# Gates of mixer B by blocks of 64 channels on half of TensorE's rows, in a two-layer hybrid encoder

## The chip, the cores and the metric

The kernel runs on one core of one Trainium2 chip. The metric is the device time of one execution in microseconds (us). The core's engines are TensorE (PE in the profile, its weight loads PEld), VectorE (DVE), ScalarE (ACT), GpSimd (POOL, unused here) and SyncE (SP, which issues most DMAs). Each takes its instructions in the order of the program.

## The reference, cut to what matters

Two layers, 512 tokens, 1024 channels, float32. A layer projects the normalised input for four token mixers (A and C: grouped attention; D: dilated attention in three groups; B: a bidirectional gated linear recurrence), gates and sums their outputs, and ends with an MLP. Mixer B has 512 channels in 8 blocks of 64, and its gates are block diagonal:

```python
xh = xc.reshape(b, s, LRU_BLOCKS, LRU_BLOCK_W)            # 8 blocks of 64 channels
gl = einsum('bsnc,gncd->gbsnd', xh, gate_w) + gate_b      # g: the two gates
r, i = sigmoid(gl[0]), sigmoid(gl[1])
log_a = -8 * r * softplus(-lam); a = exp(log_a)
u = sqrt(-expm1(2 * log_a)) * (i * xc)                    # then h = a * h_before + u
```

This is done for a forward and a backward scan (`d`), each with its own gate weights, biases and `lam`.

## The kernel before, in words

Activations lie channels on partitions, tokens along the free axis, so most products are 128x128 weights against 128x512. For accuracy every matrix is split in a high and a low part (`fp32r`), and a product is three: high by high, high by low, low by high (`mm3`, lines 173 to 182: 177, 178, 179).

The weights come as a stream of chunks of 128x1024 in the order of `PLAN`: a DMA on SP (`wload`, line 102), a cast on ACT for the high part (`whi`, line 118), a subtraction on DVE for the low part (`wlo`, line 127). Three raw and three split chunks are held. `ahead` casts the next chunks when a chunk is taken; `lows` emits the subtractions after a group's products.

`phase1` makes the projections of a layer one group after the other (`group`, lines 385 to 395): 24 products into one PSUM tile, then pieces of mixer B that wait in a queue (`tick`, as many as `TICKS` says), then, after the groups that `GATES` names, the gates of a tile of 128 channels of mixer B. Tile 0 follows the first half of the second query group of mixer C, tile 1 the first half of D's query group 0, tile 2 and tile 3 the first and second half of D's key group 1. PSUM tiles come from three tags in turn (`wide`, line 165: mm, s, t), each with two buffers. Two projections together make a rotary (`rope`, lines 331 to 365: four products with the tables on DVE, line 338, reading both PSUM tiles, then sums, line 361, and DMAs to DRAM, line 363), so the first PSUM tile of a pair is held until after the second.

`gates_b` (lines 598 to 667) does the gates of tile f: four times (two scan directions by two gates) three products of a block-diagonal 128x128 weight, half of it zeros, with the tile's convolved input, and one tanh on ACT with the bias (line 619), which reads 128x512 from PSUM. What follows is queued as `s1` to `s6`: tanh, exp and square on ACT (lines 628 to 630), products on DVE (636, 637), a square root on ACT (642), the scan on DVE (648), sums (652, 653), and the split of the result (654 on ACT, 657 on DVE). The GeLU branch puts line 591 (tanh, ACT) and line 594 (DVE) in the same queue. Both gate tiles f and f+1 use one chunk of weights, `BG`.

After the projections come the values of A and C, then mixer A's attention, whose keys and queries are loaded back from DRAM (lines 769, 773) and whose first score product is line 786. The order on every engine is the order of this program.

Of the kernel before, what the change touches and what calls it, by code (L numbers as in the profile page):

```python
# [11 lines left out]
F32 = mybir.dt.float32  # L12
F32R = mybir.dt.float32r
I32 = mybir.dt.int32
AF = mybir.ActivationFunctionType
ALU = mybir.AluOpType
AX = mybir.AxisListType
PSUM = bass.MemoryType.PSUM
# [10 lines left out]
V_GMIX, V_GMLP, V_GB, V_CW, V_CB, V_LGB, V_LAM, V_G, V_SINK = 0, 8, 16, 48, 64, 68, 84, 92, 96  # L29
NV = 104  # L30
# [4 lines left out]
# attention of A and C: the stages of a step and how many steps each lags behind the first  # L35
# [4 lines left out]
# steps of an attention phase, steps of its fill, steps of the fill ahead of the first one  # L40
MG = ((35, 48, 3), (41, 73, 2), (18, 47, 12))
# waits in the end of mixer D, in steps of the fill beside it, and the steps of that fill
E1, E2, E3, FN = (1, 5, 2, 15)
# products that warm the tensor engine up; parts in which the first two chunks come
WU, P0, P1 = (16, 2, 2)
# the order of the projections; pieces of mixer B after each; projections that its gates follow
# [25 lines left out]
PLAN = layer_plan()  # L72
# [3 lines left out]
class Body:  # L76
# [29 lines left out]
    def parts(self, i):  # L106
        """the first chunk is worked on in parts, for an early start"""
        n = (P0, P1, 1)[min(i, 2)]
        return [slice(p * (1024 // n), (p + 1) * (1024 // n)) for p in range(n)]
# [20 lines left out]
    def ahead(self, i):  # L130
        """the high parts of the next groups, and the loads beyond them"""
        i -= self.held
        n = len(self.order)
        while self.n_split < min(i + self.HLB, n):
            self.whi()
        while self.n_load < min(self.n_lo + self.RAWB, n):
            self.wload()
# [5 lines left out]
    def take2(self, *key):  # L143
        """two chunks that stay for several groups"""
        return [self.take(*key, u, wide=u) for u in range(2)]
# [38 lines left out]
    def several(self, keys, mv, cuts):  # L184
        """the groups of some chunks, side by side: each part of the depth for all of them"""
        sts = [self.wst(self.take(*key, wide=u)) for u, key in enumerate(keys)]
        pss = [self.wide() for _ in keys]
        mm = self.nc.tensor.matmul
        for k0, k1 in zip((0,) + cuts, cuts + (KD,)):
            for st, ps in zip(sts, pss):  # L190
                for k in range(k0, k1):
                    (sh, sl), (mh, ml) = st(k), mv(k)
                    mm(ps, sh, mh, start=(k == 0), stop=False)
                    mm(ps, sh, ml, start=False, stop=False)
                    mm(ps, sl, mh, start=False, stop=(k == KD - 1))
        self.ahead(self.n_take)
        self.lows()
        return pss
# [19 lines left out]
    def smt(self, n, tag):  # L218
        return self.sm.tile([128, n], F32, tag=tag, name=tag)

    def rsqrt(self, v, n, tag):
        """v: [128, n] in SBUF, positive"""
        nv = self.nc.vector
        y, t = self.smt(n, tag + "y"), self.smt(n, tag + "t")
        yi = y.bitcast(I32)
        nv.tensor_scalar(out=yi, in0=v.bitcast(I32), scalar1=1, scalar2=None, op0=ALU.logical_shift_right)
        nv.tensor_scalar(out=yi, in0=yi, scalar1=-1.0, scalar2=float(0x5F3759DF), op0=ALU.mult, op1=ALU.add)
        for _ in range(3):
            nv.scalar_tensor_tensor(out=t, in0=y, scalar=-0.5, in1=y, op0=ALU.mult, op1=ALU.mult)
            nv.tensor_tensor(out=t, in0=t, in1=v, op=ALU.mult)  # L230
            nv.scalar_tensor_tensor(out=y, in0=t, scalar=1.5, in1=y, op0=ALU.add, op1=ALU.mult)
        return y

    def xg_tile(self, xt, c, gcol):
        """xt [128, 512] f32: tile c of the residual; writes xg"""
        nc = self.nc
        nc.scalar.activation(out=self.xh[:, c], in_=xt, func=AF.Copy, scale=gcol)
        nc.vector.scalar_tensor_tensor(
            out=self.xl[:, c], in0=xt, scalar=gcol, in1=self.xh[:, c].bitcast(F32), op0=ALU.mult, op1=ALU.subtract
        )  # L240
# [10 lines left out]
    def norm_cols(self):  # L251
        """1/rms of each token, as columns [128, 4]"""
        nc = self.nc
        ps = self.misc()
        for c in range(4):
            nc.tensor.matmul(ps[:, c:c + 1], self.acc[:, c * 128:(c + 1) * 128], self.ones[:, 0:1])
        v = self.smt(4, "nv")
        nc.vector.tensor_scalar(out=v, in0=ps[:, 0:4], scalar1=1.0 / DM, scalar2=EPS, op0=ALU.mult, op1=ALU.add)
        return self.rsqrt(v, 4, "n")
# [17 lines left out]
    def setup(self):  # L277
        nc = self.nc
# [14 lines left out]
        self.d_lgb = cp.tile([128, nl, 16], F32, name="d_lgb")  # L293
# [4 lines left out]
    def derive(self):  # L298
# [5 lines left out]
        ts(out=self.d_lgb, in0=vv[:, :, V_LGB:V_LGB + 16], scalar1=0.5, scalar2=None, op0=ALU.mult)  # L304
        ts(out=self.d_nsink, in0=vv[:, :, V_SINK:V_SINK + 8], scalar1=-1.0, scalar2=None, op0=ALU.mult)
        # softplus(-lam) = max(-lam, 0) + log1p(exp(-|lam|)), log1p(u) = 2 atanh(u / (u + 2))
        n = DEPTH * 8
        sh = lambda t: t.rearrange("p (l n) -> p l n", l=DEPTH)
        lam = self.smt(n, "spl")
        ts(out=sh(lam), in0=vv[:, :, V_LAM:V_LAM + 8], scalar1=1.0, scalar2=None, op0=ALU.mult)  # L310
        mx, u, d, s, s2, p = (self.smt(n, "sp" + c) for c in "mudsqp")
# [18 lines left out]
    # ================= projections of the mixers, and mixer B =================  # L330
    def rope(self, X1, X2, T, dst, split, perm=False):
        """X1, X2 in PSUM; T: the factors (of x1, of x2 in the first half; of x2, of x1 in the second)"""
# [64 lines left out]
    def phase1(self, l):  # L397
# [27 lines left out]
        def head_scale(key, nh, sel, n=128):  # L425
            """1/rms of each head and token, but for the token's own factor: [128, 4 * nh]"""
# [21 lines left out]
        # the tokens' 1/rms, as columns, as a row, and over all partitions  # L448
# [12 lines left out]
        # tokens in other orders: by 64 from 64 on for the first group of D, by residues for the others  # L461
# [47 lines left out]
        # queries of C, queries and keys of D; gates of mixer B between them  # L509
# [18 lines left out]
    def values_ac(self):  # L528
        """values of A and C: token-major, [hi | lo]"""
# [68 lines left out]
    def gates_b(self, f):  # L598
        """gates of a tile of mixer B; what follows goes to the queue"""
# [9 lines left out]
        Tg = {}  # L609
        for d in range(2):  # L610
            for gate in range(2):
                ps = self.wide()
                o = ((f % 2) * 4 + d * 2 + gate) * 128
                st = lambda k: (hl[0][:, o:o + 128], hl[1][:, o:o + 128])
                mv = lambda k: (xch[f][:, 0], xch[f][:, 1])
                self.run(self.mm3(ps, st, mv, 1))
                t = p1.tile([128, S], F32, tag=("btr", "bti")[gate], name="btg", bufs=4)
                i = (d * 2 + gate) * 4 + f
                ns.activation(out=t, in_=ps, func=AF.Tanh, scale=0.5, bias=self.d_lgb[:, l, i:i + 1])
                Tg[f, d, gate] = t  # L620
        bs = {}
# [11 lines left out]
        def s2(f, d):  # L633
            q, a, u = bs[f, d]
            # 1 - a^2 = tanh(-log a) (1 + a^2)
            nv.scalar_tensor_tensor(out=q, in0=Tg[f, d, 0], scalar=1.0, in1=q, op0=ALU.add, op1=ALU.mult)
            nv.scalar_tensor_tensor(out=u, in0=u, scalar=1.0, in1=self.xcs[f], op0=ALU.add, op1=ALU.mult)
# [61 lines left out]
    # ================= gates and projections of the branches =================  # L699
# [44 lines left out]
    # ================= attention =================  # L744
    def pipeline(self, steps, order):
        """steps: dicts of stages; order: (stage, its distance in steps from the first)"""
# [7 lines left out]
    def attn_gqa(self, l, which, y):  # L754
        """8 heads, 2 key heads. A: all keys; C: a band, with sinks"""
# [274 lines left out]
    def attn_d_end(self, y):  # L1030
        """the groups' weights: exp(m_g - M) / sum_g l_g exp(m_g - M)"""
# [57 lines left out]
    def merge(self, a, b, na, nb, first=0):  # L1089
        """a's first step, a few of b, then na steps of a spread over nb of b; then the rest"""  # L1090
# [19 lines left out]
    # ================= the layer =================  # L1110
    def layer(self, l):
# [99 lines left out]
        def last(h):  # L1211
            """the last two tiles and the final norm, by halves of the tokens"""
# [118 lines left out]
def _pack_weights(i):  # L1331
# [13 lines left out]
    for l in range(DEPTH):  # L1345
# [3 lines left out]
        for key in PLAN:  # L1349
# [19 lines left out]
            elif k == "BG":  # L1369
                c = np.zeros((128, 8, 128), np.float32)  # L1370
                for f in range(2):
                    for d in range(2):
                        for g in range(2):
                            for h in range(2):
                                s = slice(64 * h, 64 * h + 64)
                                c[s, f * 4 + d * 2 + g, s] = gw[d, g, (2 * a[0] + f) * 2 + h]
# [15 lines left out]
def _pack_vectors(i):  # L1392
# [3 lines left out]
    for l in range(DEPTH):  # L1396
# [6 lines left out]
        v[:, V_LGB:V_LGB + 16] = i["lru_gate_b"][l].reshape(16, 128).T  # L1403
        v[:, V_LAM:V_LAM + 8] = i["lru_lambda"][l].reshape(8, 128).T
# [63 lines left out]
```

## Time and profile before

| | us |
|---|---|
| median of 3 runs | 2096.09 |
| lowest and highest run | 2095.13, 2098.7 |
| span of the profiled execution | 2091.4 |
| TensorE busy | 2071.0 (99%) |
| DVE busy | 1273.3 (61%) |
| ACT busy | 977.9 (47%) |

The span runs from the first to the last instruction of one profiled execution; the profile gives no other time of that execution, and the runs, taken without a profile, have medians 4.7 us above the span. Times in rows are counted from the start of the span. Busy times of TensorE are modelled from starts, since products overlap; the distance from start to start is the rate.

### The profile page before, as it was taken

How to read it: one execution, taken by the hardware profiler on the slowest of the kernel's cores; microseconds unless marked ns; L12 is line 12 of the kernel's file. 1: busy time of each engine (PE TensorE's matmuls, PEld its weight loads, DVE VectorE, ACT ScalarE, POOL GpSimd, SP SyncE). 2: the span in 40 equal slices, each digit the busy share in tenths (PEclk: the TensorE clock that was granted, in tenths of full speed). 3: DMA queues.
4: the chain of work that ended last, by engine and by line, in shares of the span. 5: the costliest groups of instructions: out<-in, count | busy, mean ns of one | idle time of the engine just before them, and what ended most of it. 6: DMA issues, size and time to landing. Idle time of an engine off the chain costs nothing.

```text
span 2091.4 us, 25718 instructions
## 1 busy us (share of the span) xinstructions
PE 2071.0 (99%) x9800; PEld 1711.7 (82%) x9800; DVE 1273.3 (61%) x2274; ACT 977.9 (47%) x1703; POOL 0.2 (0%) x4
## 2 busy tenths in 40 slices
PE   9999999999999999999999999999999999999997
PEld 7888889987778888888878888898877788888886
DVE  6889774575466544444658887736644665444445
ACT  4366885663534332322323667757545343322322
POOL 0000000000000000000000000000000000000000
PEclk9999999999999999999999999999999999999999
DMA  5445313122234222222325552312321432223221
GB/s 190 156 142 159 113 54 100 59 97 95 72 100 144 95 97 94 97 93 99 133 95 171 159 163 67 101 66 66 121 81 53 135 117 93 99 93 99 93 100 61
DMA packets 83407, 220.74 MB, mean 106 GB/s; under 512 B 15674, under 2 KB 17850, under 8 KB 83284
## 3 DMA queue, kind: packets, MB, share of 16 engines
q1 hardware_dynamic: 80404, 214.91, 31.6%
q10 hardware_dynamic: 2880, 4.20, 0.6%
q8 instruction: 77, 1.26, 0.3%
q14 instruction: 46, 0.38, 0.1%
HBM read 197.94 MB, written 21.12 MB: 105 GB/s over the span
## 4 chain that ended last, share of the span: by engine, by line
PE 96%; DVE 2%; ACT 1%; issue 1%; DMA 0%; SPq 0%; DVEq 0%; ACTq 0%
PE ps_mm L177 15%; PE ps_mm L179 14%; PE ps_mm L178 14%; PE ps_t L177 6%; PE ps_t L179 6%; PE ps_t L178 6%; PE ps_s L177 6%; PE ps_s L179 6%; PE ps_s L178 6%; PE ps_o L846 2%; PE ps_t L825 2%; PE ps_s L786 1%; PE ps_s L787 1%; PE ps_o L992 1%; PE ps_t L966 1%; PE ps_s L917 1%
## 5 line engine op out<-in xcount | busy, mean ns | idle before, releaser
L118 ACT CAST whi<-raw 128x1024 fp32r<-128x1024 f32 (+1 forms) x318 | 329.9, 1042 | 353.6 <-PE ps_mm L178 122.0
L127 DVE TENSOR_TENSOR wlo<-raw,whi 128x1024 fp32r<-128x1024 f32 (+1 forms) x318 | 385.0, 1214 | 106.0 <-ACT whi L118 103.3
L177 PE MATMUL ps_mm<-xh,whi 128*128 128x512 f32 x720 | 288.2, 400 | 0.0
L179 PE MATMUL ps_mm<-xh,wlo 128*128 128x512 f32 x720 | 282.0, 392 | 0.0
L178 PE MATMUL ps_mm<-xl,whi 128*128 128x512 f32 x720 | 281.8, 391 | 0.0
L177 PEld LDWEIGHTS ps_mm<-xh,whi 128*128 128x128 f32 x720 | 135.5, 188 | 32.4 <-issue 4.1
L179 PEld LDWEIGHTS ps_mm<-xh,wlo 128*128 128x128 f32 x720 | 135.6, 188 | 29.3
L178 PEld LDWEIGHTS ps_mm<-xl,whi 128*128 128x128 f32 x720 | 135.8, 189 | 26.9
L177 PE MATMUL ps_t<-xh,whi 128*128 128x512 f32 x368 | 143.7, 390 | 0.0
L178 PE MATMUL ps_t<-xl,whi 128*128 128x512 f32 x368 | 143.2, 389 | 0.0
L179 PE MATMUL ps_t<-xh,wlo 128*128 128x512 f32 x368 | 143.2, 389 | 0.0
L177 PE MATMUL ps_s<-xh,whi 128*128 128x512 f32 x352 | 138.6, 394 | 0.0
L179 PE MATMUL ps_s<-xh,wlo 128*128 128x512 f32 x352 | 137.1, 389 | 0.0
L178 PE MATMUL ps_s<-xl,whi 128*128 128x512 f32 x352 | 137.0, 389 | 0.0
L835 DVE TENSOR_TENSOR PT<-ps_t,PT 128x512 fp32r<-128x512 f32 (+2 forms) x128 | 75.2, 588 | 72.2 <-ACT PT L832 56.6
L832 ACT CAST PT<-ps_t 128x512 fp32r<-128x512 f32 (+2 forms) x128 | 63.8, 501 | 57.5 <-PE ps_o L846 56.1
L819 ACT ACTIVATE P<-P,al 128x512 f32<-128x512 f32 (+2 forms) x128 | 82.7, 646 | 12.6 <-DVE al L818 11.6
L709 DVE TENSOR_TENSOR gt<-ps_mm,rb 128x512 f32<-128x512 f32 x54 | 37.2, 688 | 80.7 <-PE ps_mm L179 80.5
L177 PEld LDWEIGHTS ps_t<-xh,whi 128*128 128x128 f32 x368 | 69.1, 188 | 17.4 <-issue 3.0
L179 PEld LDWEIGHTS ps_t<-xh,wlo 128*128 128x128 f32 x368 | 69.1, 188 | 14.4
L178 PEld LDWEIGHTS ps_t<-xl,whi 128*128 128x128 f32 x368 | 69.1, 188 | 14.3
L177 PE MATMUL ps_mm<-whi,xh 128*128 128x256 f32 (+1 forms) x224 | 79.6, 355 | 0.0
(423 smaller groups left out, 4330.7 us busy)
## 6 DMA issues: line engine op xcount, KB each, us to landing
raw<-in_w_dram SPq DMA_DIRECT2D x314, 512.0 KB, 3.5
qsA<-stk SPq DMA_DIRECT2D x32, 128.0 KB, 2.3
qsC<-stk SPq DMA_DIRECT2D x32, 128.0 KB, 2.3
K<-ks SPq DMA_DIRECT2D x16, 256.0 KB, 5.6
Q<-qsA SPq DMA_DIRECT2D x16, 256.0 KB, 4.0
Q<-qsC SPq DMA_DIRECT2D x16, 256.0 KB, 2.7
qD<-stkf SPq DMA_DIRECT2D x24, 128.0 KB, 2.2
kD<-stkf SPq DMA_DIRECT2D x24, 128.0 KB, 2.2
```

Source lines behind the costliest of these rows:

```text
L118: self.nc.scalar.copy(hi[:, s], self.raws[i][:, s])
L127: self.nc.vector.tensor_tensor(out=lo[:, s], in0=raw[:, s], in1=hi[:, s].bitcast(F32), op=ALU.subtract)
L177: mm(ps, sh, mh, start=(k == 0), stop=False)
L178: mm(ps, sh, ml, start=False, stop=False)
L179: mm(ps, sl, mh, start=False, stop=(k == n - 1))
L709: nv.tensor_tensor(out=g, in0=ps, in1=self.rb, op=ALU.mult)
L786: nc.tensor.matmul(ps[:, 0:n], qq, Kt[j][:, 0, b0 * 128:b1 * 128], start=True, stop=False)
L819: ns.activation(out=P[:, 0:n], in_=P[:, 0:n], func=AF.Copy, scale=ls)
L825: nc.tensor.transpose(pt[:, b * 128:(b + 1) * 128], P[:, b * 128:(b + 1) * 128], self.ident)
L832: ns.copy(st["dst"][0], st["src"])
L835: nv.tensor_tensor(out=st["dst"][1], in0=st["src"], in1=st["dst"][0].bitcast(F32), op=ALU.subtract)
L846: nc.tensor.matmul(o, a, b, start=(n_ == 0), stop=(n_ == len(mm) - 1))
```

## The change

A tile's two blocks of 64 channels are no longer one block-diagonal product. Block b uses the rows 64b to 64b+63 of TensorE alone, with a weight of 64x128 whose 128 columns hold both gates of that block, and writes a PSUM tile of its own; for each direction the three products of the two blocks alternate between the two PSUM tiles. For the second block the two gates stand in swapped order. Each PSUM tile then holds both gates of one block, so an eviction reads 64 partitions: for each gate two activations of 64x512 in place of one of 128x512, for one of the gates from the other half of the partitions. The weights of a chunk `BG` fill 512 columns instead of 1024; only those are loaded, cast and subtracted. The bias vectors get a second copy in the swapped order, and small temporaries of the set-up get one buffer instead of three. (Comments that only fall away are left out.)

```diff
 def parts(self, i):
+    if PLAN[self.order[i][1]][0] == "BG":
+        return [slice(0, 512)]
...
-V_GMIX, V_GMLP, V_GB, V_CW, V_CB, V_LGB, V_LAM, V_G, V_SINK = 0, 8, 16, 48, 64, 68, 84, 92, 96
-NV = 104
+V_GMIX, V_GMLP, V_GB, V_CW, V_CB, V_LGB, V_LGI, V_LAM, V_G, V_SINK = 0, 8, 16, 48, 64, 68, 84, 100, 108, 112
+NV = 120
...
-    def smt(self, n, tag):
-        return self.sm.tile([128, n], F32, tag=tag, name=tag)
+    def smt(self, n, tag, bufs=3):
+        return self.sm.tile([128, n], F32, tag=tag, name=tag, bufs=bufs)
...
-        self.d_lgb = cp.tile([128, nl, 16], F32, name="d_lgb")
+        self.d_lgb = cp.tile([128, nl, 32], F32, name="d_lgb")
...
-        ts(out=self.d_lgb, in0=vv[:, :, V_LGB:V_LGB + 16], scalar1=0.5, scalar2=None, op0=ALU.mult)
+        ts(out=self.d_lgb, in0=vv[:, :, V_LGB:V_LGB + 32], scalar1=0.5, scalar2=None, op0=ALU.mult)
...
 def gates_b(self, f):
...
         for d in range(2):
+            o = ((f % 2) * 2 + d) * 128
+            pss = [self.wide() for _ in range(2)]
+            for n, (w, z) in enumerate(((0, 0), (0, 1), (1, 0))):
+                for b, ps in enumerate(pss):
+                    r = slice(64 * b, 64 * b + 64)
+                    nc.tensor.matmul(ps, hl[w][r, o:o + 128], xch[f][r, z], start=(n == 0), stop=(n == 2))
             for gate in range(2):
-                ps = self.wide()
-                o = ((f % 2) * 4 + d * 2 + gate) * 128
-                st = lambda k: (hl[0][:, o:o + 128], hl[1][:, o:o + 128])
-                mv = lambda k: (xch[f][:, 0], xch[f][:, 1])
-                self.run(self.mm3(ps, st, mv, 1))
                 t = p1.tile([128, S], F32, tag=("btr", "bti")[gate], name="btg", bufs=4)
                 i = (d * 2 + gate) * 4 + f
-                ns.activation(out=t, in_=ps, func=AF.Tanh, scale=0.5, bias=self.d_lgb[:, l, i:i + 1])
+                for b, ps in enumerate(pss):
+                    src = slice(64 * (b ^ gate), 64 * (b ^ gate) + 64)
+                    dst = slice(64 * b, 64 * b + 64)
+                    col = i if gate == 0 else 16 + b * 8 + d * 4 + f
+                    ns.activation(
+                        out=t[dst], in_=ps[src], func=AF.Tanh, scale=0.5, bias=self.d_lgb[dst, l, col:col + 1]
+                    )
                 Tg[f, d, gate] = t
+        self.lows()
...
 # packing of the weights of a chunk BG: c is 128 x 8 x 128, of which half is used now
-                        for g in range(2):
-                            for h in range(2):
-                                s = slice(64 * h, 64 * h + 64)
-                                c[s, f * 4 + d * 2 + g, s] = gw[d, g, (2 * a[0] + f) * 2 + h]
+                        for h in range(2):
+                            for g in range(2):
+                                m = slice(64 * (g ^ h), 64 * (g ^ h) + 64)
+                                c[64 * h:64 * h + 64, f * 2 + d, m] = gw[d, g, (2 * a[0] + f) * 2 + h]
```

## Rows read from the trace of the kernel before

**Rows 1.** The page: span and instructions, busy time of TensorE

```profile
span 2091.4 us, 25718 instructions
PE 2071.0 (99%) x9800; PEld 1711.7 (82%) x9800; DVE 1273.3 (61%) x2274; ACT 977.9 (47%) x1703; POOL 0.2 (0%) x4
```

**Rows 2.** Stretches: length, busy us of PE, PEld, DVE, ACT, POOL; clock, DMA share, GB/s

```profile
133.00:171.00 38.00, 38.00 (x169) 31.33 (x168) 36.34 (x49) 26.34 (x35) 0.00 (x0) 1.00 0.52 164
...
1243.00:1247.00 4.00, 3.41 (x15) 2.86 (x16) 3.67 (x9) 3.98 (x8) 0.00 (x0) 1.00 1.07 280
```

**Rows 3.** Timeline of PE, both layers' first score product: start, length, [idle before <-releaser]

```profile
208.20 0.47 PE L786 MATMUL ps_s<-K,Q 128*128 128x512 f32 x1 [2.19 <-DMA Q<-qsA]
...
1243.59 0.47 PE L786 MATMUL ps_s<-K,Q 128*128 128x512 f32 x1 [3.43 <-DMA Q<-qsA]
```

**Rows 4.** Timeline of SP's queue, end of the projections of layer 0

```profile
200.89 1.74 SPq L363 DMA_DIRECT2D kD<-stkf  x4
```

**Rows 5.** Waits of DVE, 100 to 208 us: who for whom, us in total, times, longest

```profile
DVE wlo L127 <- ACT whi L118: 6.4, 5, 2.5
DVE yb L594 <- ACT gt L591: 3.1, 4, 1.0
DVE yB L657 <- ACT yB L654: 0.7, 1, 0.7
DVE btq L636 <- ACT btg L630: 0.7, 1, 0.7
```

**Rows 6.** Timeline of PE, tile 0 of layer 0: first gate product, first product behind it

```profile
112.26 0.40 PE L177 MATMUL ps_mm<-xch,whi 128*128 128x512 f32 x1
...
115.06 0.40 PE L177 MATMUL ps_s<-xh,whi 128*128 128x512 f32 x1
```

**Rows 7.** One tile's instructions: a copy of 64 partitions from PSUM, ns min/median/max

```profile
L853 ACT COPY yx<-ps_o x32: 577/581/586, 237.7 to 1493.9; 64x512 f32<-64x512 f32 x32
```

**Rows 8.** Timeline of ACT, around the gates of tiles 0 to 3, layer 0

```profile
118.41 0.65 ACT L591 ACTIVATE gt<-gt 128x512 f32<-128x512 f32 x1
...
128.77 0.69 ACT L619 ACTIVATE btg<-ps_mm,d_lgb 128x512 f32<-128x512 f32 x1
...
131.07 2.01 ACT L118 CAST whi<-raw 128x1024 fp32r<-128x1024 f32 x2
...
166.02 0.69 ACT L619 ACTIVATE btg<-ps_s,d_lgb 128x512 f32<-128x512 f32 x1
...
170.02 0.62 ACT L654 CAST yB<-btq 128x512 fp32r<-128x512 f32 x1 [1.58 <-DVE btq L653]
...
173.33 1.99 ACT L118 CAST whi<-raw 128x1024 fp32r<-128x1024 f32 x2
```

**Rows 9.** Timeline of DVE, layer 0: a rotary's product, and waits for ACT

```profile
107.02 0.69 DVE L338 TENSOR_TENSOR tt<-ps_s,s 128x512 f32<-128x512 f32 x1
...
119.09 0.69 DVE L594 SCALAR_TENSOR_TENSOR yb<-gt,yb 128x512 f32<-128x512 f32 x1 [1.01 <-ACT gt L591]
...
132.16 2.36 DVE L127 TENSOR_TENSOR wlo<-raw,whi 128x1024 fp32r<-128x1024 f32 x2 [2.47 <-ACT whi L118]
...
155.70 0.69 DVE L636 SCALAR_TENSOR_TENSOR btq<-btg,btq 128x512 f32<-128x512 f32 x1
...
174.40 2.36 DVE L127 TENSOR_TENSOR wlo<-raw,whi 128x1024 fp32r<-128x1024 f32 x2 [0.64 <-ACT whi L118]
```

**Rows 10.** Timeline of PE, layer 0: first product with the low weights of 132.16

```profile
134.71 0.39 PE L179 MATMUL ps_t<-xh,wlo 128*128 128x512 f32 x1
```

**Rows 11.** Timeline of PE, mixer D: from full height to 64 rows

```profile
491.13 0.39 PE L179 MATMUL ps_mm<-xh,wlo 128*128 128x512 f32 x1
491.45 1.02 PE L912 MATMUL ps_s<-Kd,Qd 64*128 64x256 f32 x4
```

**Rows 12.** Groups by shape: cast of 512 columns; subtraction, ns min/median/max with both shapes

```profile
L118 ACT CAST whi<-raw 128x512 fp32r<-128x512 f32 x4 | 2.5, 620 | 1.1 <-DMA raw<-in_w_dram 1.0
...
L127 DVE TENSOR_TENSOR wlo<-raw,whi x318: 683/1221/1253, 5.6 to 2062.4; 128x1024 fp32r<-128x1024 f32 x157, 128x512 fp32r<-128x512 f32 x2
```

More of the change, by code (lines that the diff above doesn't have):

```diff
@@ L308, in derive @@
         sh = lambda t: t.rearrange("p (l n) -> p l n", l=DEPTH)
-        lam = self.smt(n, "spl")
+        lam = self.smt(n, "spl", 1)
         ts(out=sh(lam), in0=vv[:, :, V_LAM:V_LAM + 8], scalar1=1.0, scalar2=None, op0=ALU.mult)
-        mx, u, d, s, s2, p = (self.smt(n, "sp" + c) for c in "mudsqp")
+        mx, u, d, s, s2, p = (self.smt(n, "sp" + c, 1) for c in "mudsqp")
         nv.scalar_tensor_tensor(out=mx, in0=lam, scalar=-1.0, in1=lam, op0=ALU.mult, op1=ALU.min)
@@ L1403, in _pack_vectors @@
         v[:, V_LGB:V_LGB + 16] = i["lru_gate_b"][l].reshape(16, 128).T
+        lb = i["lru_gate_b"][l][:, 1].reshape(2, 4, 2, 64)
+        for b in range(2):
+            v[:, V_LGI + 8 * b:V_LGI + 8 * b + 8] = np.tile(lb[:, :, b].reshape(8, 64).T, (2, 1))
         v[:, V_LAM:V_LAM + 8] = i["lru_lambda"][l].reshape(8, 128).T
```

## The prediction, made before the changed kernel ran

> **What bounds the kernel now.** The page first: TensorE is busy for 99% of the span [rows 1], so one reads that every product saved is time saved. The table by stages corrects that for the place of the change, the projections of a layer: there DVE is busy for 36.3 of 38 us [rows 2], nearly as full as TensorE. Which of the two sets the end of the stage is read where it ends: the first score product of mixer A waits 2.19 us in layer 0 and 3.43 us in layer 1 for a query transfer [rows 3]; TensorE had been through with the projections and values by then. That transfer stands on SP's queue behind the stores of the last rotary result, which SP issues from 200.89 [rows 4], the moment DVE has made it; from this issue to the first score product it is 7.3 us. So the phase ends with DVE. What does DVE wait for on its way? From 100 us on for nothing but ACT, 6.4 + 3.1 + 0.7 + 0.7 = 10.9 us in all, and never for TensorE [rows 5]. ACT in its turn runs in a fixed order and mostly waits for DVE. The last place where DVE is tied to a projection is the rotary at 107.02 [rows 9], which starts as its product ends. From there to 208 us DVE and ACT are one chain, and TensorE runs beside it with little to spare: the low weights that DVE begins at 132.16 are done (1.22 us each, two in 2.36) about 133.4 and wanted by the product at 134.71 [rows 9, 10], a slack of 1.3 us. The four gate steps of mixer B lie on this chain, because their evictions are ACT's.
>
> **The change part by part.**
>
> *Gate products.* There are 96 (12 for a tile of 128 channels, 4 tiles, 2 layers); 12 take 2.80 us [rows 6], all of them 22.4 us. As many are left, in pairs on separate halves of the rows. If a pair overlaps wholly a tile takes 1.4 us and 11.2 us go; if it doesn't, nothing goes. No row shows two such halves side by side. Going from full height to half costs 0.09 us: 0.32 us between starts [rows 11] in place of 0.23; I take 0.1 us for each way, as an estimate. I take the overlap, since a load already runs beside the product before it [rows 6]: their starts are 0.23 us apart at 0.40 us each, and keep the other end for the range. The Trainium skill, "TensorE: Matmul & The Clock Gate", Part 3 (packing small matmuls), states that products on different row groups run at the same time, a few ns apart; no run here shows it so far. By that rule alone the sum would be a gain, the first rival below.
>
> *Gate evictions.* Each tile had 4 activations of 128x512 and gets 8 of 64x512. The nearest row for half the partitions is a 64x512 copy from PSUM: 581 ns [rows 7]. One behind the other, the activations of the gates follow each other at 0.575 us (four from 128.77 to 131.07 [rows 8]). So each tile costs ACT 4 x 0.575 = 2.3 us more, 9.2 us in a layer. The same skill's page "TensorEngine Tiling (Array Packing)", section PSUM Bottleneck, says that tiling speeds up TensorE but not the eviction of PSUM, which may then become the bottleneck; rows 7 and 8 agree. What of the 9.2 us lies on the chain, tile by tile in layer 0:
>
> 1. Tile 0. Behind its gates on ACT stands the tanh of the GeLU branch (118.41 [rows 8]), which DVE awaits idle at 119.09 [rows 9]. It comes 2.3 us later: the chain is at +2.3.
> 2. Tile 1. Behind its gates stand two high casts of weights (131.07), which DVE awaits, idle for 2.47 us, until 132.16 [rows 8, 9]. Another 2.3 us: +4.6. TensorE's product of 134.71 then has its low weights only at about 138.0; what it saved in the first two tiles is spent waiting.
> 3. Half the weights. The chunk of the gates has 512 columns to convert in place of 1024: 0.62 us on ACT for about 1.0 (two in 1.99 [rows 8]), 0.68 us on DVE for 1.22 [rows 12]. For the first chunk this lies before 107 us, and the rotary there still waits for its projection: nothing. The second saves 0.54 us of DVE ahead of 155.70, where DVE waited some 0.16 us for ACT [rows 9]; ACT is early there too. Together -0.7: +3.9. The smaller transfer itself is waited for nowhere here.
> 4. Tile 2. Its activations began at 166.02, four of them ended well before the copy at 170.02, which waited for DVE [rows 8]. Eight, begun at 169.9, end at 174.5, when the copy was due at 173.9: 0.6 more, +4.5.
> 5. Tile 3. Its first and its last gate share one buffer of PSUM (tag mm), as the other is held for the rotary until later. This buffer comes free with the seventh activation of tile 2, about 174.05. The first pair of gates is ready at 175.0, behind the copy at 175.1; now the second pair must wait for the third activation (176.95), and is ready at 177.85; its four activations end at 180.15, when the high casts begin that began at 173.33 [rows 8]. That is +6.8, and DVE, which waited for them until 174.40 [rows 9], is idle for more than 2 us.
> 6. From there to the end no step is added, and DVE still doesn't wait for TensorE: from 177.4, four projections of 24 products at 0.23 us [rows 6] end at 199.5, while the last rotary result is stored at 200.89 + 6.8 = 207.7 and its six operations of 0.69 us [rows 9] before that begin no earlier than 203.5. Queries and keys come 6.8 us later.
>
> Layer 1 runs the same program on the same shapes and also ends its phase in a wait for the queries, of 3.43 us [rows 3]; I take the same 6.8 us for it. So +13.6 us in all.
>
> *Small things.* Wider vectors and the larger product on them in the derived constants add columns to one DVE operation of under 0.2 us, beside projections. Fewer buffers for small temporaries of the set-up cost nothing, as each is used once.
>
> **Sum.** The profiled span is 2091.4 us [rows 1]; the median of the runs is 2096.09 us, 4.7 us more for what lies around the span. 2096.1 + 13.6 = **2109.7 us**, 0.65% slower. A difference of 0.2% (about 4 us) is what a measurement of this kernel can tell from none.
>
> Ends of the unknown terms. Pairs that don't overlap lengthen only step 5 on the chain (elsewhere ACT comes after TensorE anyway): two times 0.7 us, so +2.8 us in both layers; if each of these 12 products also paid 0.1 us for the change of halves, 2.4 us more, +5.2 us. If each of the 16 added activations cost its full 0.69 us [rows 8] in place of 0.575, 16 x 0.115 = 1.8 us would come on top in a layer. Towards less: if the waits in steps 4 and 5 are found elsewhere in DVE's idle time, 2.9 us a layer go, which gives 2103.9. The idle times of 4 us that TensorE gets could lower its granted clock; in the stretch with the wait of 3.43 us it was granted in full [rows 2, 3], and by step 6 TensorE has some 4 us to spare at the end, so I add nothing.
>
> **The rivals.**
> - *TensorE sets the time after all (faster).* For it: 99% busy, no wait of TensorE from 107 us to the end of the values. Then 11.2 us go, less 8 tiles with a way in and a way out at 0.1 us: 1.6; that is 9.6 us and 2086.5 us. This is what the Part 3 rule named above would make of the time. Against it: DVE never waits for TensorE while the end waits for DVE. It decides if ACT's extra work is off the chain and the end of the phase moves with TensorE. Chance 0.08.
> - *Hidden (no change).* ACT is busy for 26.3 of 38 us [rows 2] and takes the 9.2 us in its idle time; the end remains DVE's, with the 0.7 us of step 3 less in a layer: 2094.7 us. Against it: in tiles 0, 1 and 3 the work right behind the evictions is what DVE waits for. Chance 0.08.
> - *The pairs don't overlap (the change doesn't do what it says).* TensorE saves nothing; by the ends above 2112 to 2115 us, slower as well. Against it: only that nothing is shared by the two halves. Chance 0.19.
>
> **How the numbers follow.** The forecast has 0.65 and alone spans 2104 to 2114. With the third rival and both ends it is 2102 to 2117, which leaves out the first two rivals. Slower by over 0.2%: 0.65 + 0.19 = 0.84; within: 0.08; faster: 0.08.
>
> **What would show it.** In the profile after: 64 evictions of the gates (there were 32) at about 0.58 to 0.69 us; the wait of 2.47 us at the weights behind tile 1 grown to about 4.8 us; TensorE with idle time before the first product of the keys of group 0 in mixer D (some 4 us) and within the gates of tile 3; the first score product of layer 0 at about 215 us. Starts of paired products a few ns apart would show the overlap; 0.23 us apart, the third rival. It would be wrong if the evictions of 64 partitions take half the time, or if DVE's waits for ACT don't grow.

## The result and the profile after

The change makes the kernel slower: 2112.4 us, the median of 4 runs (2109.6 to 2112.6), beside 2096.0 us of the kernel before; the ratio is 1.0074, with a 95% interval from 1.0060 to 1.0089. The profiled execution took 2112.4 us, 1.8 of them around its span. The same 1.8 us lie around the span of every execution on record whose span is known, those of the kernel before included. So the profiled execution of the kernel before, with its span of 2091.4 us, took about 2093.2 us (an estimate): it was a quick one, and the 4.7 us between its span and the median are not all time around the span. The two spans differ by 19.2 us where the medians differ by 16.4; start-up alone varies by more than the 2.8 us between the two: the rotary product at 107.02 us [rows 9] stands at 110.7 us in a later profile of a program that is the same up to there. Stretches that begin behind the start-up are the safer comparison.

The page of the changed kernel, its span and engine lines, answers to [rows 1]:

```profile
span 2110.6 us, 25762 instructions
PE 2070.2 (98%) x9800; PEld 1707.6 (81%) x9800; DVE 1271.9 (60%) x2274; ACT 1000.1 (47%) x1735; POOL 0.2 (0%) x4
```

ACT has 32 instructions and 22.2 us more. TensorE has as many products and, in this sum, as much work; a busy time that runs pairs together doesn't show what they save. That is read in the timeline of TensorE at the gates of tile 0, layer 0 ([rows 6] before); columns are start, length, engine, line, operation, tiles:

```profile
113.00 0.39 PE L181 MATMUL ps_t<-xh,wlo 128*128 128x512 f32 x1
113.32 0.49 PE L619 MATMUL ps_mm<-xch,whi 64*128 64x512 f32 x1
113.32 0.49 PE L619 MATMUL ps_s<-xch,whi 64*128 64x512 f32 x1
113.65 0.39 PE L619 MATMUL ps_mm<-xch,whi 64*128 64x512 f32 x1
113.66 0.39 PE L619 MATMUL ps_s<-xch,whi 64*128 64x512 f32 x1
...
114.91 0.50 PE L179 MATMUL ps_s<-xh,whi 128*128 128x512 f32 x1
```

The two products of a pair start within 0.01 us of each other, on two banks. (So do 42 of the 48 pairs; the other six, in tile 3 of each layer, come below.) The twelve take from 113.32 to 114.91, 1.6 us in place of 2.80, with 0.32 us into the narrow products and 0.32 us out of them where 0.23 is the usual step. So the change does what it says on TensorE. The price is in ACT's timeline behind it:

```profile
117.09 0.68 ACT L628 ACTIVATE btg<-ps_mm,d_lgb 64x512 f32<-64x512 f32 x1
117.78 0.68 ACT L628 ACTIVATE btg<-ps_s,d_lgb 64x512 f32<-64x512 f32 x1
118.48 0.69 ACT L628 ACTIVATE btg<-ps_mm,d_lgb 64x512 f32<-64x512 f32 x1
...
121.97 0.68 ACT L628 ACTIVATE btg<-ps_mm,d_lgb 64x512 f32<-64x512 f32 x1
122.68 0.63 ACT L593 ACTIVATE gt<-gt 128x512 f32<-128x512 f32 x1
```

Eight activations of 64x512 last 0.68 us each, the same as 128x512 did, and follow each other at 0.695 us: they no longer overlap, where the four of before started 0.575 us apart [rows 8]. A tile's evictions take 8 x 0.695 = 5.56 us instead of 4 x 0.575 = 2.30: 3.26 us more. The waits of DVE from 100 to 215 us (who for whom, us in total, times, longest) answer to [rows 5]:

```profile
DVE wlo L129 <- ACT whi L120: 12.0, 4, 5.7
DVE yb L596 <- ACT gt L593: 6.4, 4, 4.3
DVE yB L669 <- ACT yB L666: 2.3, 1, 2.3
DVE tt L340 <- PE ps_s L181: 1.7, 1, 1.7
DVE btq L648 <- ACT btg L642: 0.7, 1, 0.7
```

DVE waits 21.4 us for ACT where it waited 10.9. The one wait for TensorE is the rotary at 107.98, where the stretch begins. Tile by tile, from DVE's timeline ([rows 9] before):

```profile
123.35 0.69 DVE L596 SCALAR_TENSOR_TENSOR yb<-gt,yb 128x512 f32<-128x512 f32 x1 [4.30 <-ACT gt L593]
...
139.69 2.36 DVE L129 TENSOR_TENSOR wlo<-raw,whi 128x1024 fp32r<-128x1024 f32 x2 [5.74 <-ACT whi L120]
...
162.65 0.69 DVE L648 SCALAR_TENSOR_TENSOR btq<-btg,btq 128x512 f32<-128x512 f32 x1
...
186.41 2.36 DVE L129 TENSOR_TENSOR wlo<-raw,whi 128x1024 fp32r<-128x1024 f32 x2 [4.11 <-ACT whi L120]
```

Against [rows 9] these starts are later by 4.26, 7.53, 6.95 and 12.01 us; 0.96 us of each is there from the start, as the rotary at 107.98 is already that late. In between stands the copy behind tile 2, 8.55 us late (178.57 on ACT against 170.02 in [rows 8]). TensorE, with less to do, waits for what it used to find ready; from its timeline and, at the end, from SP's queue:

```profile
139.71 0.80 PE L179 MATMUL ps_t<-xh,whi 128*128 128x512 f32 x1 [4.69 <-ACT whi L120]
...
177.89 0.50 PE L619 MATMUL ps_mm<-xch,whi 64*128 64x512 f32 x1 [1.64 <-ACT btg L628]
...
178.70 0.39 PE L619 MATMUL ps_t<-xch,whi 64*128 64x512 f32 x1
181.22 0.79 PE L619 MATMUL ps_mm<-xch,whi 64*128 64x512 f32 x1 [2.13 <-ACT btg L628]
...
220.37 0.47 PE L798 MATMUL ps_s<-K,Q 128*128 128x512 f32 x1 [1.84 <-DMA Q<-qsA]
...
1262.43 0.53 PE L798 MATMUL ps_s<-K,Q 128*128 128x512 f32 x1 [2.84 <-DMA Q<-qsA]
```

```profile
212.92 1.27 SPq L365 DMA_DIRECT2D kD<-stkf  x3
```

In tile 3 one half of a pair starts at 178.70 us and the other only at 181.22, when its PSUM buffer is free: the pairs of that direction are torn apart. The last rotary result is stored 12.0 us later than in [rows 4] and the first score product of layer 0 starts 12.2 us later than in [rows 3]. From the rotary's product to the first score product it is 220.37 - 107.98 = 112.4 us, before 208.20 - 107.02 = 101.2; in layer 1 by the same count 113.5 and 102.4. That is +11.2 and +11.1 us: the slowdown arises there, in both layers alike. It comes to 22.3 us, more than the medians differ by, so some time comes back elsewhere. The place is the second product of layer 0's MLP. Stretches of 40 us within it (length, then busy us and count of PE, PEld, DVE, ACT, POOL; granted clock, DMA share, GB/s), first of the kernel before, then of the changed one:

```profile
776.00:816.00 40.00, 40.00 (x173) 32.18 (x172) 19.19 (x24) 8.94 (x9) 0.00 (x0) 1.00 0.29 95
```

```profile
790.00:830.00 40.00, 40.00 (x179) 33.11 (x177) 20.10 (x24) 8.95 (x9) 0.00 (x0) 1.00 0.28 100
...
1831.00:1871.00 40.00, 40.00 (x173) 32.22 (x172) 19.33 (x23) 8.82 (x9) 0.00 (x0) 1.00 0.28 94
```

TensorE is full in each, at the full clock, and gets through 179 products in place of 173, but in layer 0 alone. Their starts are 0.2267 us apart (mean of 765 steps) against 0.2333: 768 products make 5.1 us. Nothing of the change touches this product.

### The profile page after: what moved, and what is told of

Same layout as the page of the kernel before. It is cut to its first block, busy times and chain, and to the rows that moved or that the text cites. A ratio compares the mean times of both kernels' runs of the same rounds, so it can differ in the third digit from the quotient of the medians.

```text
span 2110.6 us, 25762 instructions
## 1 busy us (share of the span) xinstructions
PE 2070.2 (98%) x9800; PEld 1707.6 (81%) x9800; DVE 1271.9 (60%) x2274; ACT 1000.1 (47%) x1735; POOL 0.2 (0%) x4
## 4 chain that ended last, share of the span: by engine, by line
PE 90%; ACT 4%; DVE 3%; DMA 1%; issue 1%; SPq 1%; DVEq 0%; ACTq 0%
PE ps_mm L179 14%; PE ps_mm L181 14%; PE ps_mm L180 14%; PE ps_t L179 6%; PE ps_t L181 6%; PE ps_t L180 5%; PE ps_s L179 5%; PE ps_s L181 5%; PE ps_s L180 5%; PE ps_o L858 2%; PE ps_t L837 2%; ACT btg L628 2%; PE ps_s L798 1%; PE ps_s L799 1%; PE ps_o L1004 1%
## 5 line engine op out<-in xcount | busy, mean ns | idle before, releaser
L179 PEld LDWEIGHTS ps_t<-xh,whi 128*128 128x128 f32 x368 | 69.8, 190 | 31.7 <-ACT whi L120 10.2
L179 PEld LDWEIGHTS ps_s<-xh,whi 128*128 128x128 f32 x352 | 67.1, 191 | 17.8 <-issue 3.4
```

## The experiments

Times are medians; each stands beside runs of the kernel before on the same chip (2095.7 to 2097.2 us). "Phase" is the stretch from the rotary's product near 107 us to the first score product, and the same in layer 1: 101.2 and 102.4 us before, 112.4 and 113.5 us with the change.

### The sizes alone

```
-V_LGB, V_LAM, V_G, V_SINK = 68, 84, 92, 96;  NV = 104
+V_LGB, V_LGI, V_LAM, V_G, V_SINK = 68, 84, 100, 108, 112;  NV = 120
-d_lgb = cp.tile([128, nl, 16])
+d_lgb = cp.tile([128, nl, 32])
-lam = self.smt(n, "spl");  ... self.smt(n, "sp" + c)
+lam = self.smt(n, "spl", 1);  ... self.smt(n, "sp" + c, 1)
```

> The kernel before with only the sizes of the change: 16 more bias columns per layer, d_lgb twice as wide, the softplus temporaries with one buffer each; the gates stay as they were. Theory (placement): in the changed kernel the second product of layer 0's MLP ran at 0.2267 us from start to start in place of 0.2334, 768 times, because its moving tile h lies elsewhere; so the same 5.1 us go here, to about 2091 us (2090 to 2092.5), and layer 1's h products stay at 0.233. Rival (the pace came from the changed gates, by the times at which other work falls): 2096 us, and h at 0.233 in both layers.

Measured: 2089.3 us, a little under the range expected, ratio 0.9968 (0.9955 to 0.9981), phases 100.9 and 102.0 us. Layer 0's stretch has the 178 products, layer 1's has not:

```profile
780.00:820.00 40.00, 40.00 (x178) 33.15 (x177) 19.55 (x23) 8.72 (x9) 0.00 (x0) 1.00 0.31 94
1810.00:1850.00 40.00, 40.00 (x174) 32.18 (x173) 19.17 (x24) 8.93 (x9) 0.00 (x0) 1.00 0.31 98
```

So the time that comes back belongs to the sizes, which move h in SBUF by 640 bytes, and not to the gates. The gates themselves cost 2112.4 - 2089.3 = 23.1 us, which is the 11.5 us by which each phase grows (112.4 - 100.9 and 113.5 - 102.0).

### Four evictions instead of eight, products of the change

```
-for b, ps in enumerate(pss):
-    ns.activation(out=t[dst], in_=ps[src], ..., bias=self.d_lgb[dst, l, col:col + 1])
+ns.activation(out=t, in_=pss[gate], ..., bias=self.d_lgb[:, l, i:i + 1])
```

> The changed kernel with four activations of 128x512 for each tile in place of eight of 64x512: PSUM tile 0 goes whole to the first gate and tile 1 to the second, so the gates of the second block of each pair are exchanged; products, banks and weights stay those of the change. Theory (the evictions are the whole slowdown, and what TensorE saves is worth nothing): the before time, less 0.7 us a layer for the half weights, less 5.1 us in layer 0's MLP: about 2089.5 us (2088 to 2092). Rival 1 (TensorE bounds the phase after all and the evictions hide its gain): 4.8 us a layer less than that, about 2081 us. Rival 2 (the pairs themselves or their two banks cost something): 2095 us or more.

Measured: 2088.6 us, phases 100.5 and 101.6 us. The whole slowdown is gone with the added evictions, and DVE's waits for the casts, 12.0 us in the changed kernel, fall back to about what they were:

```profile
DVE wlo L129 <- ACT whi L120: 5.2, 4, 2.5
```

Beside the run with the sizes alone the difference is 0.4 us a phase and 0.7 us in the time. Pairs and half weights are all there, so together they bring no more than this, which the runs can't tell from nothing: what TensorE saves is worth next to nothing here.

### Eight evictions, products and weights of before

```
-ns.activation(out=t, in_=ps, ..., bias=self.d_lgb[:, l, i:i + 1])
+for b in range(2):
+    r = slice(64 * b, 64 * b + 64)
+    ns.activation(out=t[r], in_=ps[r], ..., bias=self.d_lgb[r, l, i:i + 1])
```

> The sizes of the change, with the kernel before's full-height products and full weights, but each eviction in two activations of 64x512 that stay on their own partitions. Theory (eight evictions instead of four are the slowdown): 11.8 us a layer on the chain and 1.2 us at each attention start, on 2091 us: about 2116 us (2113 to 2118), if their pace is 0.695 us also without a change from one half of the partitions to the other; if only an activation that reads one half and writes the other loses the overlap, the pace is 0.575 us and the time about 2107 us (2105 to 2110). Rival (row-tiled products, not evictions): 2091 us.

Measured: 2114.7 us, phases 112.4 and 114.5 us: 25.4 us more than the sizes alone, with not one product changed. Here no activation goes from one half of the partitions to the other, and the pace is 0.697 us all the same (ACT's timeline; x2 stands for two in a row, low half and high half of one bank):

```profile
117.43 1.38 ACT L621 ACTIVATE btg<-ps_mm,d_lgb 64x512 f32<-64x512 f32 x2
118.82 1.39 ACT L621 ACTIVATE btg<-ps_s,d_lgb 64x512 f32<-64x512 f32 x2
```

### The order of the halves

Three kernels, each executed once, on why the overlap is gone. The lists are (gate, block) for the first two, (half, gate) for the third; each is reversed in the second direction.

```
the read half first:     ((0, 0), (1, 1), (0, 1), (1, 0))[:: 1 - 2 * d]
the written half first:  ((0, 0), (1, 0), (0, 1), (1, 1))[:: 1 - 2 * d]
no crossing, low low high high (products of before):
                         ((0, 0), (0, 1), (1, 1), (1, 0))[:: 1 - 2 * d]
```

> The changed kernel, its four activations of a direction in another order: the two that read the low half of the PSUM partitions, then the two that read the high half, and the other direction reversed, so that of the 7 steps from one activation to the next within a tile the half that is read changes in 2 and the half that is written in 4. Theory A (a step that changes the half that is read costs the overlap of 0.12 us with the activation before): 5 of 7 steps at 0.575 us, 2 at 0.695. Theory B (the half that is written): 3 of 7 at 0.575. Theory C (either): 1 of 7, the one between the two directions. Theory D (activations of 64 partitions out of PSUM do not overlap, whatever their halves): all at 0.695 us and the time unchanged. By A 0.6 us less a tile, about 2109 us; by B and C 2110 to 2112; by D 2112 us.

> The changed kernel, its four activations of a direction ordered by the half that is written (low, low, high, high, and the other direction reversed): the half that is written changes in 2 of 7 steps, the half that is read in 4. Theory A (read half): 3 of 7 steps at 0.575 us. Theory B (written half): 5 of 7. Theory C (either): 1 of 7. Theory D: all at 0.695 us.

> The kernel of the run with evictions in halves, but the four activations of a direction in the order low, low, high, high (the other direction high, high, low, low): an activation reads and writes the same half as the one before it in 5 of 7 steps. Theories A to C (a change of half costs the overlap): 5 of 7 steps at 0.575 us, 0.6 us less a tile and about 2111 us. Theory D (64 partitions out of PSUM): all at 0.695 us and about 2114.7 us.

Median steps between the eight activations of a tile, in us: the read half first 0.693, 0.692, 0.697, 0.589, 0.686, 0.695, 0.691; the written half first 0.693, 0.706, 0.699, 0.584, 0.679, 0.695, 0.698; no crossing 0.585, 0.685, 0.588, 0.572, 0.572, 0.691, 0.586. In the first two only the fourth step is short, the one at which neither half changes; in the third the five at which the half stays. ACT's timeline of the first and the third, the fourth step of each:

```profile
120.67 0.69 ACT L626 ACTIVATE btg<-ps_mm,d_lgb 64x512 f32<-64x512 f32 x1
121.26 0.67 ACT L626 ACTIVATE btg<-ps_t,d_lgb 64x512 f32<-64x512 f32 x1
```

```profile
118.82 0.67 ACT L623 ACTIVATE btg<-ps_mm,d_lgb 64x512 f32<-64x512 f32 x1
119.40 0.67 ACT L623 ACTIVATE btg<-ps_t,d_lgb 64x512 f32<-64x512 f32 x1
```

So theory C holds: an activation starts about 0.11 us ahead of the end of the one before only if both the half that it reads and the half that it writes are the same as that one's. The third run took 2109.3 us, phases 110.8 and 111.6, against 112.4 and 114.5 in the order low, high: 1.6 and 2.9 us a phase for 20 steps of 0.11 us (five in each of four tiles, 2.2 us). The first two took 2114.6 and 2110.9 us, where 2110 to 2112 was expected of theory C: one run each is too few to price one step, so theory C rests on the steps.

### Where h lies

Addresses in these runs are those of the built programs, in bytes within a partition. In all kernels whose weights aren't moved, xh and the weight tiles whi and wlo start 64 bytes past a multiple of 256.

```
 hp = pool(es_m, f"h{l}")
+hp.tile([128, (128, 160)[l] // 4], F32, tag="pad", name="pad")    # first run
+hp.tile([128, (64, 224)[l] // 4], F32, tag="pad", name="pad")     # second run
```

> The kernel before with an unused pad ahead of h in the pool of the MLP, 128 bytes per partition in layer 0 and 160 in layer 1, so that h starts 64 bytes past a multiple of 256 in both layers, as it does in layer 0 of the changed kernel and as xh does in all of them (layer 1's h starts 32 past one in the changed kernel, 160 in the kernel before). Theory (the address modulo 256 sets the pace): h at 0.227 us in both layers, 2 x 768 x 0.0067 = 10.2 us less, about 2086 us. Rival 1 (something else of layer 0): 2091 us, layer 0 alone. Rival 2 (the address is not it): 2096 us.

> The kernel before with other pads ahead of h: 64 bytes in layer 0, so that h starts at a multiple of 256, and 224 in layer 1, so that it starts 128 past one. Theory 1 (only 64 past a multiple of 256 is fast): h at 0.233 us in both layers, 2096 us. Theory 2 (a multiple of 128 is fast too): 0.227 us in both, 2086 us. Theory 3 (only a multiple of 256): 0.227 us in layer 0 alone, 2091 us.

The first took 2087.6 us, ratio 0.9957 (0.9941 to 0.9974), with the fast pace in both layers:

```profile
780.00:820.00 40.00, 40.00 (x178) 33.10 (x178) 19.55 (x23) 8.83 (x9) 0.00 (x0) 1.00 0.30 94
1810.00:1850.00 40.00, 40.00 (x178) 33.14 (x177) 19.69 (x24) 8.97 (x9) 0.00 (x0) 1.00 0.32 98
```

The second, one run, took 2092.0 us and fits none of the three theories: a multiple of 256 is slow, and 128 past one lies in between.

```profile
776.00:816.00 40.00, 40.00 (x173) 32.07 (x172) 19.18 (x24) 8.90 (x9) 0.00 (x0) 1.00 0.31 99
1813.00:1853.00 40.00, 40.00 (x176) 32.81 (x176) 19.91 (x24) 8.95 (x9) 0.00 (x0) 1.00 0.31 101
```

Is it the operand's own address, or how it lies to the weights'? Two kernels, each executed once, move the weights. They start from the kernel before with the softplus temporaries in one buffer each (this frees 896 bytes) and 32 unused bytes ahead of layer 1's h, so that xh and both h lie 64 bytes past a multiple of 256 ahead of any move:

```
+pd = pool("pd"); pd.tile([128, 32], F32, name="pd")      # ahead of whi, wlo: both runs
 self.hlp = pool("hlp", self.HLB)
+pe = pool("pe"); pe.tile([128, 32], F32, name="pe")      # behind them: first run alone
```

> The same for h alone, with the weight tiles whi and wlo moved by 128 bytes against all moving operands. Theory (the moving operand's own address sets the pace): xh and h at 0.227 us, about 2086 us. Rival (it is the moving operand's address relative to the weights'): xh and h at 0.233 us or some other pace, about 2110 us.

> As the run with the weights moved by 128 bytes, but xh and both h moved by the same 128, so that weights and moving operands all start 192 bytes past a multiple of 256. Theory 1 (a product is at its fastest when its moving operand and its weights start at the same place modulo 256): xh and h at 0.227 us again, about 2086 us. Theory 2 (both must start 64 past a multiple of 256): xh and h at 0.232 us or more, about 2113 us, as in that run.

With the weights alone moved: 2112.8 us, and the slower pace in h and in xh. With all three moved: 2083.6 us and the fast pace again. Stretches of layer 0's second product and of the projections, of the one and the other:

```profile
785.00:825.00 40.00, 40.00 (x174) 32.44 (x173) 19.55 (x23) 8.63 (x9) 0.00 (x0) 1.00 0.31 93
...
60.00:100.00 40.00, 40.00 (x190) 32.95 (x189) 34.56 (x75) 14.50 (x20) 0.00 (x0) 1.00 0.49 150
```

```profile
777.00:817.00 40.00, 40.00 (x178) 33.15 (x177) 19.55 (x23) 8.71 (x9) 0.00 (x0) 1.00 0.31 94
...
60.00:100.00 40.00, 40.00 (x194) 33.67 (x193) 35.24 (x75) 14.87 (x20) 0.00 (x0) 1.00 0.53 161
```

My theory, the operand's own address, falls: what counts is how moving operand and weights lie to each other. In all these runs the pace of h, xh and mh was 0.227 us where both start at the same place modulo 256, and 0.229 to 0.234 where not. With the weights alone moved, the products of xh were 2% slower and the phases took 102.8 and 103.5 us, against 100.5 and 101.6 with all three moved: about 2% more as well. Within layer 0's phase ACT then waits 1.5 us for TensorE, against 0.2. So a faster TensorE gains next to nothing in these phases, but a slower one seems to cost: it has little to spare, as the prediction read. The way of these 2 us to the end of the phase was not followed.

### A version that beats both

The kernel before, its gates untouched, with this carried to the other full-width operands:

```
+mhp.tile([128, 40], F32, name="padr")                           # beside mh, ml
+self.y0p.tile([128, 56], F32, tag="pady", name="pady")          # ahead of yB, yA, yC, yD
+if l == 1: hp.tile([128, 32 // 4], F32, tag="pad", name="pad")  # ahead of layer 1's h
+lam = self.smt(n, "spl", 1);  ... self.smt(n, "sp" + c, 1)      # frees 896 bytes
```

> The kernel before with its addresses moved so that every full-width moving operand but xch starts 64 bytes past a multiple of 256: the softplus temporaries with one buffer each (this frees 896 bytes), and unused pads of 224 bytes ahead of yB (it moves yA, yC and yD too), 160 beside mh and 32 ahead of layer 1's h. Gates as before the change. Theory (the address sets the pace, and TensorE bounds these phases): 10.2 us from the two h as in the run with pads, 2 x 192 products of mh at 0.0076 us less (2.9 us) and 2 x 336 of the y tiles at 0.0067 us less (4.5 us, if the attention phases are bound by TensorE): 2078 to 2082 us. Rival (the pace depends on something else in those phases, or something else bounds them): 2086 us.

Measured: 2077.7 us, just under the range expected, the median of 5 runs (2074.8 to 2081.6), ratio 0.9912 (0.9897 to 0.9926): 18.9 us faster than the kernel before beside it and 34.7 faster than the changed one. The product of mh has the fast pace as well; the same stretch of the kernel before, then of this one:

```profile
643.00:683.00 40.00, 40.00 (x173) 32.15 (x172) 25.74 (x33) 17.28 (x25) 0.00 (x0) 1.00 0.27 92
```

```profile
642.00:682.00 40.00, 40.00 (x178) 33.14 (x177) 26.93 (x36) 17.72 (x25) 0.00 (x0) 1.00 0.31 98
```

From mh's first product to h's it is 131.5 us in both layers in place of 133.0. The y tiles run faster too (0.227 to 0.230 against 0.233), but from the first score product to mh's first it is 432.4 and 433.6 us where it was 433.3 and 433.1: there the gain doesn't reach the time, so this part of the expectation failed. The rows account for some 13 us (10.2 of h, 3.0 of mh), and the two profiled executions differ by 11.7 us (spans of 2091.4 and 2079.7 us). The first, at some 2093.2 us, stands 3.4 us under the median of its kernel and the second, at 2081.5, 3.8 us over: that is the rest of the 18.9, and what makes executions of one kernel differ by so much stays open.

## Why the prediction was right

Forecast 2109.7 us, measured 2112.4. The mechanism is the one forecast: evictions on the chain of DVE and ACT, in a phase that TensorE doesn't bound. Removing them alone takes the whole loss away, adding them alone makes it. But two terms were mis-sized, with opposite signs, and nearly cancelled: the phases lost 22.3 us instead of 13.6, and some 6 us came back in a place that the prediction didn't look at. That the number came within 3 us was in part luck. (The sum starts from the median of the runs, so its reading of the 4.7 us as time around the span did no harm.)

- **Gate products.** They overlap, as taken; the third rival is out. The rule of the Trainium skill, "TensorE: Matmul & The Clock Gate", Part 3, holds in this trace: pairs start 0.01 us apart or less, but for the second direction of tile 3, where one half waits for its PSUM buffer. The way into the narrow products and out of them costs 0.09 us each, as estimated. The gain that would follow from the rule alone, the first rival, did not come: with four evictions those products are worth 0.7 us.
- **Gate evictions, the term that failed.** The prediction put four more activations at 0.575 us, 2.3 us a tile, and as the upper end let the added four cost their full 0.69. In fact the four that were there lose their overlap as well: 8 x 0.695 - 4 x 0.575 = 3.26 us. The nearest row, a copy at 581 ns [rows 7], and the step of 0.575 us [rows 8] seemed to agree; but the activations last 0.68 us on half the partitions too, and the step came from activations of 128 partitions, none of which changes the partitions that it reads or writes. The Trainium skill, "ScalarE: Activation LUTs", section What ACT_TABLE_LOAD costs, says that activations one behind the other overlap by about 93 ns. The trace agrees where the half stays (0.11 us) and not where it changes (none).
- **Step 1**, +2.3: measured 4.26 - 0.96 = +3.30 us. **Step 2**, +2.3: +3.27; DVE's wait behind tile 1 is 5.74 us, not 4.8, and TensorE stands idle for 4.69 us ahead of the keys of group 0, as said. **Step 3**, -0.7: 6.95 - 7.53 = -0.6, as said.
- **Step 4**, +0.6: 8.55 - 6.95 = +1.6, the size of the evictions again. **Step 5**, +2.3: 12.01 - 8.55 = +3.46. The wait was found where it was put: the first direction of tile 3 waits 1.64 us for a buffer of PSUM and the second 2.13, and ACT then has to wait for the second, as its timeline shows ahead of the fifth eviction of the tile:

```profile
181.19 0.68 ACT L628 ACTIVATE btg<-ps_s,d_lgb 64x512 f32<-64x512 f32 x1
182.54 0.68 ACT L628 ACTIVATE btg<-ps_t,d_lgb 64x512 f32<-64x512 f32 x1 [0.67 <-PE ps_t L619]
```

- **Step 6** held: nothing is added from there to the end, and from the last store to the first score product it is 7.45 us where it was 7.3. The five steps sum to 3.30 + 3.27 - 0.6 + 1.6 + 3.46 = 11.0 us a layer instead of 6.8. So the first score product of layer 0 came at 220.37 us and not at about 215.
- **The clock**, put at nothing: the granted clock does fall, as the stretches of the changed kernel show.

```profile
133.00:171.00 38.00, 33.27 (x143) 26.16 (x143) 31.47 (x44) 28.02 (x38) 0.00 (x0) 0.96 0.47 141
...
141.00:144.00 3.00, 3.00 (x9) 2.46 (x10) 2.32 (x4) 2.97 (x5) 0.00 (x0) 0.65 0.49 188
...
181.00:184.00 3.00, 2.78 (x8) 1.84 (x9) 1.31 (x3) 2.28 (x5) 0.00 (x0) 0.50 0.01 3
...
222.00:226.00 4.00, 4.00 (x13) 3.13 (x12) 3.96 (x8) 3.97 (x6) 0.00 (x0) 0.62 0.93 261
```

After the wait of 4.69 us it is 0.65 of full speed on the mean of three us, and 0.50, the lower of its two levels, after the two waits in tile 3. Of this, the chain shows no more than the 0.67 us of ACT's wait there. At the start of the attention the dip costs little: from the first score product to mh's first it is 435.7 and 433.9 us after the change, 433.3 and 433.1 before, and 433.7 and 434.1 in the run with evictions in halves, which has the phase of the change. No run separates this term.
- **Small things, costed at nothing:** the sizes. The sentence counted their instructions, and these do cost nothing; it did not ask what the sizes do to the addresses of all that lies behind. They gave 6.4 us (4 to 9), of which the rows show 5.1. The sum as measured is 2096.0 + 22.3 - 5.1 = 2113 us.

## What to carry to other kernels

Before saving work on the engine that is 99% busy, read which engine ends the phase: here 1.2 us of TensorE a tile were bought with 3.3 us on ACT, and only ACT's were on the path. Yet an engine with little to spare can come onto the path when it gets slower, as the run with the moved weights suggests. Splitting an eviction into halves costs more than the count of instructions, as neighbours that change their partitions lose their overlap; if it must be, keep neighbours on the same half. And an edit of a tile's size is an edit of every address behind it: compare two kernels at equal addresses, or a layout that moved by chance passes for an effect of the change.

## What the runs showed of the hardware that was not expected

- Activations out of PSUM on 64 partitions take 0.68 us, as on 128, and overlap by 0.11 us only if the half read and the half written are both those of the activation before.
- A 128x512 fp32r product of h has a step of 0.2267 us where its moving operand and its weights start at the same place modulo 256 bytes (64 and 64, or, in one run, 192 and 192); elsewhere h, xh and mh take 0.229 to 0.2343 us. The y tiles at the same place as the weights took 0.227 to 0.230 us. The offset alone doesn't give the pace: h 128 bytes off the weights ran at 0.2333 us in the kernel before and at 0.2324 with the weights moved. What in the chip makes this was not tried.
- TensorE kept its full clock through a wait of 3.43 us in the kernel before [rows 2, 3] and lost it after 4.69 us, and after 1.64 and 2.13 us close together, in the changed one. The length of the last wait doesn't decide it: ahead of layer 0's first score product the wait was 2.19 us before [rows 3] and 1.84 us after the change, and only after the shorter one did the clock fall, to a mean of 0.62 (shown above, from 222 us), where before it was

```profile
209.00:213.00 4.00, 4.00 (x19) 3.31 (x18) 3.86 (x9) 3.98 (x8) 0.00 (x0) 1.00 1.05 286
```
